# Splitting the down projection's second unit into up's buffers, ahead of up's last sums

## The chip, the cores and the metric

The kernel runs on one core of a Trainium2 chip. The metric is the device time of one execution in microseconds (us); of several runs the median is taken. All times inside an execution are counted from the start of the profiled span.

Engines are called as the profile calls them: PE is TensorE (matmuls), DVE is VectorE, ACT is ScalarE, POOL is GpSimd, SP is SyncE, which here only issues DMAs. ACT and POOL issue DMAs too.

## The reference

One encoder layer over two requests, 512 + 256 = 768 tokens of width 2048, in fp32. A Fourier group and a windowed attention group are mixed and projected, and then comes the part that matters here:

```python
h = rmsnorm(x, ln_mlp_g)
u = relu(h @ w_up)            # (768, 2048) @ (2048, 8192)
x = x + (u * u) @ w_down      # (768, 8192) @ (8192, 2048)
y = rmsnorm(x, ln_final_g)
```

The outputs are the two requests' `y`, fp32.

## The kernel before

Every fp32 product is made of three matmuls in the PE's faster fp32 format. Each factor is split in two, a high part (`wh` for weights, `sh` for the left factor: a copy of the fp32 tile into that format, on ACT) and a low part (`wl`, `sl`: the tile minus its high part, on DVE). A product is high x high + high x low + low x high.

Both projections of the MLP use a Strassen-like scheme with seven products instead of eight, so the factors are sums and differences of quarter matrices.

**Up.** 32 units (numbered 0 to 31, `UL` is the last) of seven steps. In a step, PE makes one of the seven products of the unit (`up_product`), while ACT and DVE prepare the factors of later steps (`up_high`, `up_low`, `up_sum`) and take the results of the previous step (`up_out`): DVE adds the product from PSUM to a partial sum (line 909, "the take"), and in the second half of the units ACT applies relu and square (lines 916 and 917). The four results of a unit are the quarters C11, C12, C22, C21, which end with steps 1, 5, 4 and 6. `up_after` then makes the sums of these quarters that down needs as left factors: C11+C22 after the last step, C12-C11 three steps later, C21-C22 and C11+C21 four steps later. Each is made on DVE (line 923) into one of three `sm` buffers and stored to DRAM (`sd`); in the last unit POOL issues those stores, before it ACT does. For the last unit these later steps fall into the start of down. C12's square is stored too (`a`, line 919).

**Down.** 112 units: two halves of seven products (in the order 4, 2, 6, 0, 1, 3, 5) of eight units each. A unit has one left factor (two of 128 x 384) and two weight tiles of 128 x 1024. `loads(u)` issues the unit's DMAs on SP: the left factor from DRAM (`sr`, line 1128) and the weight tiles (`down_piece`, line 1061). `sums(u)` makes the weight sums where the product needs them, and the high parts (ACT: two `wh` at line 1142, then `sh` at line 1146). `lows(u)` makes the low parts (DVE: two `wl` at line 1152, then `sl` at line 1153). `products(u)` is 36 matmuls on PE (line 1163): for three blocks of rows, two halves of columns, two weight tiles and three terms. In the loop, unit `u` is worked on while unit `u+1`'s `lows`, unit `u+2`'s `sums` and unit `u+3`'s `loads` are issued.

The first eight units of down use product 4, whose weight tiles are kept: they are needed again in later products. `down_piece` puts the kept tiles 0 and 1 into the weight pool's two `raw` buffers (in the profile: `rw`), 2 and 3 into two buffers `re`, and all others into sixteen buffers `rd`.

**Buffers.** Up has a pool of its own, `up`, with four weight buffers `ur` (16 KB per partition in all), two `sx`, ten `o` and three `sm`. It is closed after the last sums, and down's pool `ep` is laid over the same memory: `re` and `sr` over the `ur` buffers, the result tiles `acc0` to `acc11` over `sx`, `o` and `sm`. The buffers `rd` lie over the right factor of up, `xf`, which PE reads until up's last product. A tile laid over another is written only after the last reader of the old one. There are four `wh` and four `wl` buffers in a pool that both stages share.

Unit 0 of down is prepared while up still runs: `loads(0)` at step 3 of the last unit, `sums(0)` and `lows(0)` at step 5. Its left factor is held in three `o` buffers of up (in the profile `osr`, `osh`, `osl`), since the pool `ep` does not exist yet.

**Order.** The order on PE, ACT and DVE is the order of the code. SP and POOL are ordered by the planner at compile time, by when it expects an instruction's inputs and buffers to be ready. The code around the seam, with `up_out(UL, 6)` as the take of C21:

```python
    products(0, ps, 0)
    up_out(UL, 6)
    for m in (1, 2):
        products(0, ps, m)
    for s in (3, 4):
        up_after(UL, s)
    up_ctx.close()
    tctx.close()
```

After it `loads(1)`, `loads(2)` and `sums(1)` follow, and the loop of down starts with `loads(3)` and `lows(1)`. POOL loads the residual into `acc0` to `acc11` (line 1238), four DMAs of 256 KB in each of the loop's iterations 1 to 6.

Of the kernel before, what the change touches and what calls it, by code (L numbers as in the profile page):

```python
# [11 lines left out]
F32 = mybir.dt.float32  # L12
# [8 lines left out]
P = 128  # L21
# [19 lines left out]
def hybrid_encoder(ctx: ExitStack, tc: tile.TileContext, a: dict):  # L41
# [3 lines left out]
    def f32(ap):  # L45
        return ap.bitcast(F32)
# [104 lines left out]
    with ExitStack() as ph:  # L151
# [319 lines left out]
        for pair, c0 in enumerate([0, 256, 512, 768, 2048, 1024, 1280, 1536, 1792]):  # L471
            ps = [[pp.tile([P, 512], F32, tag="ps", name="pz") for _ in range(2)] for _ in range(2)]
            for j in range(4):
                wh, wl = wpiece(w_in[:, 4 * j : 4 * j + 4, c0 : c0 + 256], 4, 256)
# [191 lines left out]
    for u in range(len(units)):  # L666
        t = pace * u
# [258 lines left out]
    def up_out(u, s):  # L926

        if units[u][0] == 0:
            q, bank, how = ((C11, "X", "copy"), (C11, "Z", "add"), (C12, "X", "copy"), (C22, "Y", "copy"), (C22, "X", "add"), (C12, "Y", "add"), (C21, "X", "copy"))[s]
            up_take(u, q, bank, how)  # L930
            if s in (1, 4, 5, 6):
                up_put(u, q)
            return
        q, bank = ((C11, "X"), (C11, "Z"), (C12, "X"), (C22, "Y"), (C22, "X"), (C12, "Y"), (C21, "X"))[s]
        up_take(u, q, bank, "add")
        if s in (1, 4, 5, 6):
            up_relu2(u, q, {C11: s_d[2], C22: s_d[3], C12: a21_d}.get(q))

    def up_after(u, s):


        if u < 0 or units[u][0] == 0:
            return
        if s == 0:
            up_left(u, 0, C11, C22, ALU.add)
        elif s == 3:
            up_left(u, 5, C12, C11, ALU.subtract)
        elif s == 4:
            up_left(u, 6, C21, C22, ALU.subtract)
            up_left(u, 4, C11, C21, ALU.add)  # L950
            for q in range(4):
                del uo[u, q]
# [94 lines left out]

    def down_piece(k, q, h, keep=False):  # L1050

        kk = k % HP
        apart = kk // 4 == (0 if (q, h) == (1, 1) else 1 if (q, h, keep) == (0, 0, True) else -1)
        if apart and kk % 4 < 2:
            raw = wpool.tile([P, 1024], F32, tag="raw", name="rw", bufs=2)
        elif apart:
            raw = ep["p"].tile([P, 1024], F32, tag="re", name="re", bufs=2)
        else:
            raw = ep["p"].tile([P, 1024], F32, tag="rd", name="rd", bufs=16)
        r0 = (4 * (k // 2) + 2 * q + k % 2) * P  # L1060
        nc.sync.dma_start(raw[:], a["w_down"][r0 : r0 + P, h * 1024 : (h + 1) * 1024])
        return raw

    def right_load(i, k):


        if i == 4:
            kept[k] = down_piece(k, 1, 1)
            return kept[k], None
        if i == 2:  # L1070
            return down_piece(k, 0, 1), kept[k]
        if i == 6:
            return down_piece(k, 1, 0), kept[k]
        if i == 0:
            t, kept[k] = kept[k], down_piece(k, 0, 0, True)
            return t, kept[k]
        if i == 1:
            return kept[k], None
        return (down_piece(k, 1, 0), kept[k]) if i == 3 else (down_piece(k, 0, 1), kept.pop(k))
# [35 lines left out]
    def factor_tile(u, what):  # L1115

        dt = F32R if what in ("sh", "sl") else F32
        if u == 0:
            return up.tile([P, 2, HALF], dt, tag="o", name="o" + what, bufs=10)
        return ep["p"].tile([P, 2, HALF], dt, tag=what, name=what, bufs=2 if what == "s2" else 3)  # L1120

    def loads(u):
        kh, i, j = dunits[u]
        g = kh * HP // 2 + j
        srcs = [x[g] for x in left_terms.get(i, (s_d[i],))]
        ss = [factor_tile(u, what) for what, _ in zip(("sr", "s2"), srcs)]
        for x, src in zip(ss, srcs):
            nc.sync.dma_start(x[:], src[:])
        parts[u] = [ss, [right_load(i, kh * HP + 2 * j + q) for q in range(2)]]
# [16 lines left out]
        nc.scalar.activation(sh[:], ss[0][:], AF.Copy)  # L1146
        parts[u] = [(sh, sl, ss[0]), whl]

    def lows(u):
        (sh, sl, sr), whl = parts[u]  # L1150
        for wh, wl, t in whl:
            nc.vector.tensor_tensor(out=wl[:], in0=t[:], in1=f32(wh[:]), op=ALU.subtract)  # L1152
        nc.vector.tensor_tensor(out=sl[:], in0=sr[:], in1=f32(sh[:]), op=ALU.subtract)  # L1153

    def products(u, ps, m, cols=range(2)):
# [20 lines left out]
    kept, parts, ep = {}, {}, {}  # L1176
# [3 lines left out]
    for u in range(len(units)):  # L1180
        for s in range(2 if u == 0 else 0, 7):
            up_step(u, s)
            x2_jobs.get((u, s), lambda: None)()
            if u == 0 and s == 3:
                for x in pts:
                    x1_factors(*x)
                bctx.close()
            if u == 13 and s == 0:
                xs = up_ctx.enter_context(tc.tile_pool(name="xs", bufs=1, side="right", reuse_waits="tile")).tile([P, 2, 4, HALF], F32R, tag="xs", name="xs")
                nc.gpsimd.dma_start(f32(xs[:]), x2_d[steps[0][1]][:])  # L1190
                right.append([xs])
            if u == UL and s == 3:
                loads(0)
            if u == UL and s == 5:
                sums(0)
                lows(0)
            if u == UL and s == 6:
                up_after(UL, 0)
    ps = [pp.tile([P, 2, 512], F32, tag="ps", name="pd") for _ in range(3)]
    ps = [x[:].rearrange("p a b -> p (a b)") for x in ps]  # L1200
    products(0, ps, 0)
    up_out(UL, 6)
    for m in (1, 2):
        products(0, ps, m)
    for s in (3, 4):
# [15 lines left out]
        acc[i // 2][i % 2] = epool.tile([P, 1024], F32, tag=f"acc{i}", name=f"acc{i}")  # L1221
    acc4 = lambda m, n: acc[m][n // 2][:, n % 2 * 512 : (n % 2 + 1) * 512]
    ep["gf"] = epool.tile([P, D], F32, tag="gf", name="gf")
    loads(1)
    loads(2)
    sums(1)
    behind = None
    for u, (kh, i, j) in enumerate(dunits):
        if j == 0 and u > 0:
            ps = [pp.tile([P, 2, 512], F32, tag="ps", name="pd") for _ in range(3)]  # L1230
            ps = [x[:].rearrange("p a b -> p (a b)") for x in ps]
        final = kh == 1 and i == order[-1]
        last = j == HP // 2 - 1
        if u + 3 < len(dunits):
            loads(u + 3)
        if 1 <= u <= NM:
            for n in range(4):
                nc.gpsimd.dma_start(acc4(u - 1, n), x1_d[u - 1][n][:])
        if u == NM + 1:
            nc.gpsimd.dma_start(ep["gf"][:], a["ln_final_g"].partition_broadcast(P))  # L1240
        if u + 1 < len(dunits):
            lows(u + 1)
        if final:
            for fn in beside[j]:
                fn()

        def evacuate(m, ns=None, i=i, ps=ps):
            for r, c, sign in results[i]:
                x, y = acc[3 * r + m][c][:], ps[m]
                if ns is not None:  # L1250
                    x, y = x[:, ns * 512 : (ns + 1) * 512], y[:, ns * 512 : (ns + 1) * 512]
                sc = rm if sign > 0 else nrm
                nc.vector.scalar_tensor_tensor(
                    out=x, in0=y, scalar=sc[:, 3 * r + m : 3 * r + m + 1], in1=x, op0=ALU.mult, op1=ALU.add
                )

        for m in range(3 if u > 0 else 0):

            if not (final and j >= HP // 2 - 2 and m == 2):
                products(u, ps, m)  # L1260
        if final and last:
            for n in range(2):
                for v in (u - 1, u):
                    products(v, ps, 2, (n,))

            for what, m, q in (
# [3 lines left out]
            ):  # L1270
                if what == "e":
                    evacuate(m, q - 2)
                    square(3 + m, q)
                elif what == "g":
                    for n in range(2):
                        gains(3 + m, n)
                elif what == "r":
                    row_factor(3 + m)
                else:
                    put(3 + m, q, q < 2, {(2, 0): nc.gpsimd, (2, 1): nc.scalar}.get((m, q), nc.sync))  # L1280
            parts.clear()
        if not (final and j >= HP // 2 - 2):
            del parts[u]
        if behind is not None:
            behind(2)
            behind = None
        if u + 2 < len(dunits):
            sums(u + 2)
        if last and not final:
            evacuate(0)  # L1290
            evacuate(1)
            behind = evacuate
# [58 lines left out]
```

## Time and profile before

| what | value |
|---|---|
| median of 3 runs | 2660.26 us (2658.65 to 2661.46) |
| profiled execution: span from first to last instruction | 2660.9 us |
| profiled execution: its own time | not given apart from the span |
| PE busy | 2606.8 us, 98% |
| DVE, ACT, POOL busy | 1732.0, 1060.1, 265.1 us |
| DMA | 468.31 MB, mean 176 GB/s |
| matmuls of up (line 888) | 781 to 1727 us |
| matmuls of down (line 1163) | 1726.8 to 2648 us |

How to read the lines further down. A row of the timeline is: start, duration, engine, line of the kernel, operation, output <- inputs, shapes, count; in brackets the idle time of that engine just before it, and what ended it. "ACTq" or "SPq" is the issue of a DMA on that engine's queue. A row of the chain is: start, duration, what the end of the execution waited for in that stretch. A row of the waits is: who, at which line, <- for what: total us, times, longest. In a row of stretches, the busy times of PE, PE's weight loads, DVE, ACT and POOL follow the length, each with its count, then the granted clock of PE (1.00 is full), the busy share of the DMA engines and GB/s.

### The profile page before, as it was taken

Reading aid. Unit: us, or ns where it says so; the run is one execution under the profiler, and the core shown is the slowest. Engines: PE = TensorE matmul, PEld = TensorE weight load, DVE = VectorE, ACT = ScalarE, POOL = GpSimd, SP = SyncE. Lnnn points to the kernel's source line nnn. Section 1 sums busy time; section 2 is a strip of 40 time slices with the busy share of each in tenths; the row PEclk is TensorE's granted clock in tenths of the full one; section 3 lists DMA queues with packets and bytes.
Section 4 is the critical chain, followed back from the end, with each engine's and each line's share of the span. In section 5 each row is a group of like instructions: output and inputs, shape, how many; then the busy total and the mean of one; then the engine's idle time right before and its main releaser. Section 6 shows DMA issues by size and latency. Waiting matters only on the chain.

```text
span 2660.9 us, 35017 instructions
## 1 busy us (share of the span) xinstructions
PE 2606.8 (98%) x13652; PEld 2376.5 (89%) x13652; DVE 1732.0 (65%) x2100; ACT 1060.1 (40%) x1523; POOL 265.1 (10%) x375
## 2 busy tenths in 40 slices
PE   8999998998999999998999999999999999999998
PEld 8999997877889999998999999978888888888886
DVE  6334446766746565654777777747776775777677
ACT  5233326664433333332545444433333333333335
POOL 1011212334210010101000000020000000000000
PEclk9999999999999999999999999999999999999999
DMA  5323464444664454547666666585553672554364
GB/s 172 122 93 109 140 202 146 121 127 150 205 219 159 157 188 160 182 151 278 199 227 231 212 217 230 188 326 178 178 176 99 203 255 65 180 186 157 102 206 145
DMA packets 261094, 468.31 MB, mean 176 GB/s; under 512 B 26240, under 2 KB 157824, under 8 KB 259392
## 3 DMA queue, kind: packets, MB, share of 16 engines
q1 hardware_dynamic: 196064, 304.83, 36.3%
q10 hardware_dynamic: 51792, 101.73, 9.9%
q0 software_dynamic: 13072, 59.52, 6.4%
q8 instruction: 107, 1.75, 0.3%
q14 instruction: 59, 0.48, 0.1%
HBM read 345.67 MB, written 120.32 MB: 175 GB/s over the span
## 4 chain that ended last, share of the span: by engine, by line
PE 88%; DMA 4%; DVE 3%; issue 3%; ACT 1%; POOL 1%; SPq 0%; POOLq 0%; ACTq 0%; DVEq 0%
PE pd L1163 34%; PE pu L888 32%; PE pz L481 11%; PE pm L693 6%; PE pv L186 1%; DMA ur<-in_w_up 1%; PE pa L313 1%; PE s L522 1%; PE o L596 1%; PE t L577 1%; DMA oar<-oad 0%; PE pe L334 0%; DMA ry<-zq 0%; DVE s L535 0%; ACT p L552 0%
## 5 line engine op out<-in xcount | busy, mean ns | idle before, releaser
L888 PE MATMUL pu<-xf,wh 128*128 128x384 f32 x3328 | 850.4, 337 | 8.4 <-ACT wh L868 6.8
L888 PEld LDWEIGHTS pu<-xf,wh 128*128 128x128 f32 x3328 | 601.9, 188 | 11.1 <-ACT wh L868 7.2
L888 PE MATMUL pu<-xf,wl 128*128 128x384 f32 x1664 | 559.9, 336 | 0.3 <-DVE wl L874 0.3
L1163 PE MATMUL pd<-wl,sh 128*128 128x512 f32 x1332 | 519.3, 390 | 2.7 <-DVE wl L1152 2.7
L1163 PE MATMUL pd<-wh,sl 128*128 128x512 f32 x1332 | 519.5, 390 | 1.5 <-DVE sl L1153 1.5
L1163 PE MATMUL pd<-wh,sh 128*128 128x512 f32 x1332 | 519.4, 390 | 0.0
L1142 ACT ACTIVATE wh<-rd 128x1024 fp32r<-128x1024 f32 x200 | 202.0, 1054 | 532.5 <-PE pd L1163 441.9
L1152 DVE TENSOR_TENSOR wl<-rd,wh 128x1024 fp32r<-128x1024 f32 x200 | 236.0, 1221 | 235.6 <-ACT wh L1142 235.0
L868 ACT ACTIVATE wh<-ur 128x1024 fp32r<-128x1024 f32 x160 | 169.9, 1062 | 385.2 <-PE pu L888 198.6
L888 PEld LDWEIGHTS pu<-xf,wl 128*128 128x128 f32 x1664 | 313.2, 188 | 0.8 <-DVE wl L874 0.8
L1163 PEld LDWEIGHTS pd<-wl,sh 128*128 128x128 f32 x1332 | 250.7, 188 | 55.3 <-DVE wl L1152 3.1
L1163 PEld LDWEIGHTS pd<-wh,sl 128*128 128x128 f32 x1332 | 250.7, 188 | 54.1 <-DVE sl L1153 1.8
L1163 PEld LDWEIGHTS pd<-wh,sh 128*128 128x128 f32 x1332 | 250.7, 188 | 51.9
L874 DVE TENSOR_TENSOR wl<-ur,wh 128x1024 fp32r<-128x1024 f32 x160 | 195.6, 1222 | 94.9 <-ACT wh L868 94.9
L909 DVE TENSOR_TENSOR o<-pu,o 128x768 f32<-128x768 f32 x160 | 153.0, 956 | 116.0 <-PE pu L888 112.3
L481 PE MATMUL pz<-hh,wh 128*128 128x384 f32 x576 | 147.0, 336 | 0.0
L481 PE MATMUL pz<-hh,wl 128*128 128x384 f32 x576 | 146.2, 334 | 0.0
L481 PE MATMUL pz<-hl,wh 128*128 128x384 f32 x576 | 146.1, 334 | 0.0
L1135 DVE TENSOR_TENSOR rd<-rd 128x1024 f32<-128x1024 f32 x112 | 131.8, 1218 | 0.0
L868 ACT ACTIVATE wh<-sx 128x1024 fp32r<-128x1024 f32 x64 | 67.9, 1062 | 129.2 <-PE pu L888 99.4
L66 DVE TENSOR_TENSOR wl<-raw,wh 128x1024 fp32r<-128x1024 f32 x56 | 69.0, 1236 | 66.6 <-ACT wh L65 64.0
L1153 DVE TENSOR_TENSOR sl<-sr,sh 128x768 fp32r<-128x768 f32 x111 | 105.6, 951 | 0.0
(209 smaller groups left out, 3564.5 us busy)
## 6 DMA issues: line engine op xcount, KB each, us to landing
rd<-in_w_down SPq DMA_DIRECT2D x176, 512.0 KB, 5.1
ur<-in_w_up SPq DMA_DIRECT2D x128, 512.0 KB, 3.8
sr<-sd SPq DMA_DIRECT2D x95, 384.0 KB, 5.4
pd<-o ACTq DMA_DIRECT2D x64, 384.0 KB, 2.3
o<-pd POOLq DMA_DIRECT2D x64, 384.0 KB, 6.0
sd<-sm ACTq DMA_DIRECT2D x60, 384.0 KB, 2.8
raw<-in_w_in SPq DMA_DIRECT2D x40, 512.0 KB, 3.6
raw<-in_w_out SPq DMA_DIRECT2D x32, 512.0 KB, 4.8
```

Of the source, the lines that this page charges most:

```text
L66: nc.vector.tensor_tensor(out=lo, in0=src, in1=f32(hi), op=ALU.subtract)
L481: nc.tensor.matmul(ps[c][s][:, :HALF], w[:, i, cs], h[j][:, i, s * HALF : (s + 1) * HALF], start=first and n == 0, stop=last and n == 2,)
L693: nc.tensor.matmul(ps[:], l(k), w[:, k % 2, :], start=(k == 0 and n == 0), stop=(k == 7 and n == 2))
L868: nc.scalar.activation(wh[:], raw[:], AF.Copy)
L874: nc.vector.tensor_tensor(out=wl[:], in0=raw[:], in1=f32(wh[:]), op=ALU.subtract)
L888: nc.tensor.matmul(ps[:, t, :HALF], w[:, i, t * P : (t + 1) * P], xb[:, o, i, :], start=(s == first_of[bank] and i == 0 and n == 0), stop= ...
L909: nc.vector.tensor_tensor(out=o, in0=src, in1=o, op=ALU.add)
L1135: add = lambda x, y, op: nc.vector.tensor_tensor(out=x[:], in0=x[:], in1=y[:], op=op)
L1142: nc.scalar.activation(wh[:], t[:], AF.Copy)
L1152: nc.vector.tensor_tensor(out=wl[:], in0=t[:], in1=f32(wh[:]), op=ALU.subtract)
L1153: nc.vector.tensor_tensor(out=sl[:], in0=sr[:], in1=f32(sh[:]), op=ALU.subtract)
L1163: nc.tensor.matmul(ps[m][:, ns], l[:, q, ts], w[:, ns], start=(j == 0 and q == 0 and t == 0), stop=(j == HP // 2 - 1 and q == 1 and t == 2),)
```

## The change

Unit 1 of down is prepared while up still runs, as unit 0 was.

- `loads(1)` moves to step 5 of the last unit of up, behind `lows(0)`. Its left factor goes into three more `o` buffers of up, and its two weight tiles (numbers 2 and 3) into two of up's `ur` buffers (`down_piece(..., early=True)`, tag `ur`, named `rw`).
- `sums(1)` and the first `wl` of `lows(1)` move to step 6, behind the sum C11+C22. The second `wl` and the `sl` come behind the take of C21, in front of up's last three sums.
- Tiles 2 and 3 are kept for later products, but up's buffers do not last; so they are loaded a second time into `re`, after `loads(2)`.
- The loop leaves out `lows(1)`, which is done.

```diff
@@ def down_piece
-    def down_piece(k, q, h, keep=False):
+    def down_piece(k, q, h, keep=False, early=False):
...
-        if apart and kk % 4 < 2:
+        if early:
+            raw = up.tile([P, 1024], F32, tag="ur", name="rw", bufs=4)
+        elif apart and kk % 4 < 2:
@@ def right_load
+        if i == 4 and k in (2, 3):
+            return down_piece(k, 1, 1, early=True), None
         if i == 4:
             kept[k] = down_piece(k, 1, 1)
             return kept[k], None
@@ def factor_tile
-        if u == 0:
+        if u < 2:
             return up.tile([P, 2, HALF], dt, tag="o", name="o" + what, bufs=10)
@@ def lows
-    def lows(u):
+    def lows(u, qs=range(2)):
         (sh, sl, sr), whl = parts[u]
-        for wh, wl, t in whl:
+        for wh, wl, t in [whl[q] for q in qs]:
             nc.vector.tensor_tensor(out=wl[:], in0=t[:], in1=f32(wh[:]), op=ALU.subtract)
+        if 1 not in qs:
+            return
         nc.vector.tensor_tensor(out=sl[:], in0=sr[:], in1=f32(sh[:]), op=ALU.subtract)
@@ the last unit of up
             if u == UL and s == 5:
                 sums(0)
                 lows(0)
+                loads(1)
             if u == UL and s == 6:
                 up_after(UL, 0)
+                sums(1)
+                lows(1, (0,))
...
     products(0, ps, 0)
     up_out(UL, 6)
+    lows(1, (1,))
     for m in (1, 2):
         products(0, ps, m)
@@ after up's pools are closed
-    loads(1)
     loads(2)
-    sums(1)
+    for k in (2, 3):
+        kept[k] = down_piece(k, 1, 1)
...
-        if u + 1 < len(dunits):
+        if 0 < u and u + 1 < len(dunits):
             lows(u + 1)
```

## The prediction

> **What bounds the kernel now.** I read the page's busy times first, then the chain in order of time, then PE's waits, then each engine's instructions around the place where the chain leaves PE between the up and the down projection.
>
> ```profile
> PE 2606.8 (98%) x13652; PEld 2376.5 (89%) x13652; DVE 1732.0 (65%) x2100; ACT 1060.1 (40%) x1523; POOL 265.1 (10%) x375
> ```
>
> PE is the bound, with 98% busy. So only time in which PE stands still or runs slowly can be won.
>
> ```profile
> 1728.17 7.56 DMA sd<-sm
> ...
> 1739.97 891.51 PE pd L1163 x3919
> ```
>
> This is the chain in order of time (start, us, what). At the seam it leaves PE for a store of `sm` and sums of VectorE; from 1739.97 to 2631 it is PE alone. The waits say what PE stood for (total, times, longest):
>
> ```profile
> PE pd L1163 <- DVE wl L1152: 2.7, 1, 2.7
> PE pd L1163 <- DVE sl L1153: 1.5, 1, 1.5
> ```
>
> They are PE's only waits from 1700 to 2631. The instructions of PE there:
>
> ```profile
> 1726.76 0.39 PE L1163 MATMUL pd<-wh,osh 128*128 128x512 f32 x1
> ...
> 1734.92 0.39 PE L1163 MATMUL pd<-wh,sh 128*128 128x512 f32 x1
> 1737.97 0.50 PE L1163 MATMUL pd<-wl,sh 128*128 128x512 f32 x1 [2.66 <-DVE wl L1152]
> 1739.97 0.80 PE L1163 MATMUL pd<-wh,sl 128*128 128x512 f32 x1 [1.50 <-DVE sl L1153]
> ...
> 1746.39 0.40 PE L1163 MATMUL pd<-wh,sl 128*128 128x512 f32 x1
> ...
> 1750.71 0.39 PE L1163 MATMUL pd<-wh,sh 128*128 128x512 f32 x1
> ```
>
> Unit 0 of down (36 matmuls) runs from 1726.76 to 1734.92: 8.16 us, 0.2267 each. Unit 1 runs from 1734.92 to 1750.71, the first matmul of unit 2: 15.79 us for the same 36. The seam costs **15.79 - 8.16 = 7.63 us**. Of that, 3.05 + 2.00 - 2 x 0.2267 = 4.60 is standing still, and the 15 starts from 1739.97 to 1746.39 take 6.42 instead of 3.40, 3.02 more: the clock was low.
>
> ```profile
> 1726.76:1734.92 8.16, 8.16 (x38) 6.76 (x37) 3.90 (x5) 6.50 (x8) 1.64 (x3) 1.00 0.81 252
> 1739.97:1746.39 6.42, 6.42 (x15) 5.08 (x16) 3.09 (x3) 0.00 (x0) 2.97 (x6) 0.51 0.96 355
> 1744.00:1759.00 15.00, 15.00 (x63) 12.33 (x62) 3.23 (x3) 3.35 (x4) 6.46 (x12) 0.93 1.03 418
> ```
>
> (Stretch; after the busy times the granted clock, the DMA share and GB/s.) Granted clock 1.00 before the gap, 0.51 behind it.
>
> **The change, part by part.** Why was unit 1 late? VectorE and ScalarE, in order:
>
> ```profile
> 1727.79 0.95 DVE L909 TENSOR_TENSOR o<-pu,o 128x768 f32<-128x768 f32 x1
> ...
> 1735.82 0.96 DVE L923 TENSOR_TENSOR sm<-o 128x768 f32<-128x768 f32 x1 [3.94 <-DMA sd<-sm]
> 1736.70 2.35 DVE L1152 TENSOR_TENSOR wl<-re,wh 128x1024 fp32r<-128x1024 f32 x2
> 1738.97 0.95 DVE L1153 TENSOR_TENSOR sl<-sr,sh 128x768 fp32r<-128x768 f32 x1
> ```
>
> ```profile
> 1728.80 0.33 ACTq L919 DMA_DIRECT2D a<-o  x1
> 1729.17 0.85 ACT L916 ACTIVATE o<-o 128x768 f32<-128x768 f32 x1 [0.40 <-ACT o L917]
> ...
> 1730.80 1.99 ACT L1142 ACTIVATE wh<-re 128x1024 fp32r<-128x1024 f32 x2
> 1732.69 0.83 ACT L1146 ACTIVATE sh<-sr 128x768 fp32r<-128x768 f32 x1
> 1734.44 2.00 ACT L1142 ACTIVATE wh<-rd 128x1024 fp32r<-128x1024 f32 x2 [0.92 <-PE pd L1163]
> ```
>
> Unit 1's `lows` (two `wl`, one `sl`) are queued on VectorE behind up's last sum, which waits 3.94 us for one of the three `sm` buffers, whose store lands at 1728.17 + 7.56 = 1735.73. On ScalarE its `wh` and `sh` stand behind C21's relu and square (from 1729.17).
>
> *The splits moved ahead.* On ScalarE `sums(1)` (two `wh`, one `sh`) comes in front of C21's relu and square. It can start where that relu started, 1729.17: the `wh` end at 1730.23 and 1731.17, `sh` at 1732.0. On VectorE the first `wl` follows at 1730.3 to 1731.5, the take of C21 (0.95) to 1732.4, the second `wl` to 1733.5, `sl` to 1734.4 (1.22 and 0.95 each, overlapping by some 0.08 as in the rows). PE wants them at 1734.92 (first), 1735.15 (`wl`) and 1735.37 (`sl`). So `sl` is **1.0 us early**, the others more. Gain: the 4.60, and with no gap no low clock: 3.02. I take 7.6. The new wait of the first `wl` (for 1730.23) holds the take of C21 behind it, and so C21's PSUM buffer until 1732.4; in the code the next to use it is down's second group, unit 8, due at 1792.
>
> *What moves back.* C21's relu and square (0.85 each) go from 1729.17 to 1732.4, end by 1734.1, and unit 2's `wh` still starts at 1734.44, where it waits for PE. The three last sums run 1734.4 to 1737.0; the third no longer waits, since its buffer is free at 1735.73. Behind them are unit 2's `lows`: 1737.0 plus 2.35 plus 0.95 is 1740.2. PE wants unit 2 at 1734.92 + 8.16 = 1743.08, so 2.9 us are left. GpSimd's stores of these sums go out at about 1735.3, 1736.2 and 1737.1, and its loads of `acc`, queued behind, begin as before:
>
> ```profile
> 1737.08 0.54 POOL L924 DMA_DIRECT2D sd<-sm  x1 [4.36 <-DVE sm L923]
> 1737.61 4.25 POOL L1238 DMA_DIRECT2D acc<-x  x8
> ```
>
> Four of the `acc` tiles lie over `o` buffers that unit 1 now holds until PE has done it (1743.1); their loads are the 11th and later, and at 0.53 each the 11th is due at 1742.9 at the earliest, so the hold is 0.2 us, of tiles wanted first at unit 7's end, 1792.
>
> *The moved loads.* `osr` and two `rw` of unit 1 go into up's buffers. SyncE can issue them when unit 30's last sum has freed an `o` buffer, about 1717.2; they replace one `sr` and two `re` of the same sizes. The nearest load, the `sr` of 1716.6 below, landed 6.8 us after issue: so by 1725, a few tenths of issue included; ScalarE wants them at 1729.17. Cost 0; cover 4 us.
>
> *The two tiles loaded twice.* 2 x 512 KB more. They lie over a buffer of unit 1, so SyncE holds at them until VectorE has read it (1731.5 or 1733.5), with unit 3's loads behind. This meets a stretch in which the DMA engines are full (418 GB/s, above):
>
> ```profile
> 1726.95 0.81 SPq L1061 DMA_DIRECT2D rd<-in_w_down  x2
> ...
> 1737.32 0.81 SPq L1061 DMA_DIRECT2D rd<-in_w_down  x2
> ```
>
> Loads issued near 1716, 1737 and 1743, with the time from issue to landing:
>
> ```profile
> L1128 SPq DMA_DIRECT2D sr<-sd x1: 327/327/327, 1716.6 to 1716.6; - x1
> DMA to landing us min/median/max: 6.8/6.8/6.8
> L1061 SPq DMA_DIRECT2D rd<-in_w_down x2: 328/380/433, 1737.3 to 1737.7; - x2
> DMA to landing us min/median/max: 4.3/5.4/6.6
> L1061 SPq DMA_DIRECT2D rd<-in_w_down x2: 457/470/482, 1743.5 to 1744.0; - x2
> DMA to landing us min/median/max: 13.0/14.0/15.0
> ```
>
> Unit 2's tiles (1726.95) stand ahead of the reload and keep their time. Unit 3's second tile lands at 1737.7 + 6.6 = 1744.3, unit 5's at 1744.0 + 15.0 = 1759.0; between them come 2 x (2 x 512 + 384) KB (the tiles' sizes by the code), so SyncE's queue gets 196 GB/s: 7.4 us for a unit that PE works on for 8.16. From below, the reload fits before 1737.6 and costs 0. From above, its 1 MB is moved at 196 GB/s ahead of unit 3: 5.3 us, landing 1749.6; then `wh` 1.06, `wl` 1.22 and `sl` 0.88 reach 1752.8, where PE wants `sl` at 1734.92 + 2 x 8.16 + 0.45 = 1751.7: PE stands 1.1 us. Later units gain 0.8 each. I take 0, since SyncE waited until 1737.32 before and now has unit 3's loads ready to go some 2 us sooner.
>
> The trace has the split by row; a page has it by rule. The Trainium skill, "DMA: Bandwidth & Descriptors", section on queues, rings and completion order, says that each DMA engine takes turns between the queues that have work, packet by packet. Half of 418 would be 209 GB/s, an estimate from that rule; by it the reload costs 5.0 us of lead, and the sum stays the same within the 1.1 us above.
>
> *The rest* (buffer names, the order of `lows`) costs nothing: the number of sums and activations is unchanged.
>
> Sum: -4.60 - 3.02 + 0 = **-7.6 us**. The profiled span of 2660.9 stands 0.6 above the median of the runs, 2660.26; against the median this is **2652.6 us** (-0.29%). About 0.2%, 5.3 us, is what a measurement of this kernel can tell from no change.
>
> **The rivals.** *Unit 3 or 4 starved.* Reload and bunched stores push unit 3 later than the bound above: issued at 1736 with the 15.0 us of unit 5's tile it lands at 1751.0, `sl` is there at 1754.2, and PE stands 2.5 us. A short stand costs itself only:
>
> ```profile
> 1269.07 0.59 PE L888 MATMUL pu<-xf,wh 128*128 128x384 f32 x2 [1.52 <-issue]
> ...
> 1269.67 0.51 PE L888 MATMUL pu<-xf,wh 128*128 128x384 f32 x2
> ```
>
> After 1.52 us of standing the next pairs take 0.59 and 0.51, the usual time. So 2655.1. For it: the full DMA engines. Against it: 196 GB/s is more than PE uses, and unit 3's second tile landed 1758.9 - 1744.3 = 14.6 us ahead of its PE time.
>
> *The moved loads late, a wait in the place of the one removed.* If unit 1's tiles, issued at 1718.4, took those 15.0 us, they land at 1733.4, the `wh` end at 1735.4, `sl` at 1737.5: PE stands 2.2 us, 2654.8. Against it: DMA has room there, and the rows show 6.8.
>
> *Slower: the queue order.* SyncE's order is left to the compile-time planner. If it puts the reload ahead of unit 2's tiles, these go out at 1733.9 instead of 1726.95. The point that decides: PE then stands from 1743.8 (second tile), low clock adds 3.0, and the gain is gone once it stands over 4.6 us, when the tiles land after some 1746. At the longest landing of any `rd` load (the last number),
>
> ```profile
> DMA to landing us min/median/max: 3.0/5.1/17.2
> ```
>
> 17.2 us, they land at 1751.1, the products can go on at 1753.4, PE stands 9.6, and 9.6 + 3.0 - 7.6 = +5.0: 2665.3. Against it: in the code unit 2's loads come first, and the reload is ready later.
>
> A sentence apart: the Trainium skill, "TensorE: Matmul & The Clock Gate", Part 1, gives a cold stretch of about 3.4 us at half rate, an estimated loss of 1.7 where the rows have 3.02; by the page the gap would be worth 6.3 instead of 7.6, and the rows decide.
>
> **How the numbers follow.** Forecast 0.70, unit 3 starved 0.12, moved loads late 0.06, queue order 0.07, unforeseen of either sign 0.05. The forecast's own range is 2651.2 to 2654.2 (the runs spread 1.4 to either side). The range is 2651.0 to 2657.0: it takes in both partial gains and leaves out the queue order, the unforeseen and the forecast's lower edge. Faster by over 0.2% (below 2654.9): 0.70, half of the two partial cases, 0.09, less 0.01: 0.78. Within 0.2%: the other half and most of the queue order, whose 2665.3 lies at that bound: 0.15. Slower: 0.07.
>
> **What would show it.** In the profile after: PE's waits at its L1163 gone; unit 1 as long as unit 0 (8.16 us); granted clock near 1.00 through the seam; `wl` of unit 1 read from `rw`, ahead of the last three sums; the last sum without its wait for a store; unit 2's `sl` done by about 1740; from 1744 on everything 7.6 us earlier. The prediction is wrong if PE stands at unit 2, 3 or 4 for `wl` or `wh` behind a late `rd`, or if a low clock shows behind a gap that I have at zero.

## The result, and the profile after

Over eight runs of each, the changed kernel takes 2653.78 us (2651.6 to 2654.89) and the kernel before 2659.88 (2657.5 to 2662.11). The ratio is **0.9975, with a 95% interval of 0.9966 to 0.9985**: faster by 6.6 us by the ratio, between 4 and 9, and by 6.1 us by the medians. A second series gave 2653.34 against 2659.08, ratio 0.9976 (0.9967 to 0.9984).

The forecast was 2652.6, range 2651 to 2657. The question was where a gain of this size comes from, and whether the reload gives part of it back.

The page and the chain after:

```profile
span 2651.5 us, 35021 instructions
...
PE 2602.9 (98%) x13652; PEld 2374.7 (90%) x13652; DVE 1726.5 (65%) x2100; ACT 1059.8 (40%) x1523; POOL 264.1 (10%) x375
```

```profile
1267.23 457.86 PE pu L888 x2640
1725.09 896.93 PE pd L1169 x3957
```

The chain (start, us, what) now runs from up into down without leaving PE. PE has no wait at all between 1690 and the end of down's products. Units 0, 1 and 2 of down, as stretches, starting at down's first matmul:

```profile
1724.93 0.39 PE L1169 MATMUL pd<-wh,osh 128*128 128x512 f32 x1
```

```profile
1724.93:1733.09 8.16, 8.16 (x38) 6.76 (x37) 5.77 (x7) 6.62 (x8) 0.55 (x1) 1.00 0.84 278
1733.09:1741.25 8.16, 8.16 (x38) 6.76 (x36) 5.19 (x6) 2.26 (x3) 4.28 (x8) 1.00 0.98 339
1741.25:1749.41 8.16, 8.16 (x38) 6.76 (x36) 3.32 (x3) 3.26 (x4) 3.22 (x6) 1.00 1.02 418
```

Unit 1 takes 8.16 us where it took 15.79, PE is busy throughout, and the granted clock stays at 1.00. VectorE at the seam:

```profile
1728.43 1.23 DVE L1156 TENSOR_TENSOR wl<-rw,wh 128x1024 fp32r<-128x1024 f32 x1 [2.39 <-ACT wh L1146]
1729.58 0.95 DVE L909 TENSOR_TENSOR o<-pu,o 128x768 f32<-128x768 f32 x1
1730.45 1.21 DVE L1156 TENSOR_TENSOR wl<-rw,wh 128x1024 fp32r<-128x1024 f32 x1
1731.58 0.95 DVE L1159 TENSOR_TENSOR osl<-osr,osh 128x768 fp32r<-128x768 f32 x1
1732.45 2.69 DVE L923 TENSOR_TENSOR sm<-o 128x768 f32<-128x768 f32 x3
1735.05 2.35 DVE L1156 TENSOR_TENSOR wl<-rd,wh 128x1024 fp32r<-128x1024 f32 x2
1737.33 0.95 DVE L1159 TENSOR_TENSOR sl<-sr,sh 128x768 fp32r<-128x768 f32 x1
```

Unit 1's three low parts end at 1732.53, ahead of the three sums, which run back to back: the wait for a store is gone.

**A measure that leaves out the scatter.** Down's first matmul starts at 1726.76 in the profile before and at 1724.93 after, though PE's work ahead of it is the same; over all profiles of this study it lies between 1723.28 and 1728.30, in no order with the kernels. Why it scatters is not known. So I compare the stretch from that matmul to the end of the span: 2660.9 - 1726.76 = 934.1 before, 2651.5 - 1724.93 = 926.6 after, **7.5 us less**. The stretch has a scatter of its own, mostly from the low clock behind a stand of PE: the kernel before gave 933.3 in a second profile (6.7 us), and kernel b, further down, 929.3 to 931.0. All kernels on this measure (the two columns on the left are the row of the first matmul and the page's span):

```
kernel                                   first     span    stretch  over the change   ratio (95%)
before                                   1726.76   2660.9  934.1    +7.5              1
before, again                            1723.99   2657.3  933.3    +6.7              -
the change                               1724.93   2651.5  926.6     0                0.9975 (0.9966-0.9985)
the change, again                        1728.30   2654.8  926.5    -0.1              0.9976 (0.9967-0.9984)
a: free buffer for the last sum          1727.09   2654.3  927.2    +0.6              0.9982 (0.9973-0.9990)
f: a, and low parts reordered            1725.20   2652.0  926.8    +0.2              0.9982 (0.9973-0.9991)
b: low parts behind the sums             1725.93   2656.9  931.0    +4.4              0.9991 (0.9982-1.0000)
b again                                  1724.27   2653.6  929.3    +2.7              -
b a third time                           1727.18   2658.2  931.0    +4.4              -
c: reload after unit 7's loads           1723.28   2649.8  926.5    -0.1              0.9979 (0.9970-0.9987)
d2: two more tiles loaded                1727.55   2660.5  933.0    +6.4              1.0003 (0.9994-1.0012)
d4: four more tiles loaded               1725.21   2662.1  936.9    +10.3             1.0017 (1.0008-1.0027)
e: reload ahead of unit 2's loads        1724.20   2655.1  930.9    +4.3              0.9988 (0.9979-0.9998)
```

### The profile page after: what moved, and what is told of

It is laid out like the page before. It is cut to its first block, busy times and chain, and to the rows that moved or that the text cites. A ratio compares the mean times of both kernels' runs of the same rounds, so it can differ in the third digit from the quotient of the medians.

```text
span 2651.5 us, 35021 instructions
## 1 busy us (share of the span) xinstructions
PE 2602.9 (98%) x13652; PEld 2374.7 (90%) x13652; DVE 1726.5 (65%) x2100; ACT 1059.8 (40%) x1523; POOL 264.1 (10%) x375
## 4 chain that ended last, share of the span: by engine, by line
PE 90%; DMA 3%; DVE 3%; POOL 1%; ACT 1%; issue 1%; SPq 0%; POOLq 0%; ACTq 0%; DVEq 0%
PE pu L888 34%; PE pd L1169 34%; PE pz L481 11%; PE pm L693 6%; PE pv L186 1%; DMA ur<-in_w_up 1%; PE pa L313 1%; PE o L596 1%; PE s L522 1%; DMA ofr<-ofd 1%; PE t L577 1%; PE pe L334 0%; ACT p L552 0%; DMA oar<-oad 0%; PE ptx L131 0%
## 5 line engine op out<-in xcount | busy, mean ns | idle before, releaser
L1169 PE MATMUL pd<-wh,sh 128*128 128x512 f32 x1320 | 513.5, 389 | 0.0
L1169 PE MATMUL pd<-wl,sh 128*128 128x512 f32 x1320 | 513.5, 389 | 0.0
L1169 PE MATMUL pd<-wh,sl 128*128 128x512 f32 x1320 | 513.5, 389 | 0.0
```

The costliest lines, as they stand in the source:

```text
L1169: nc.tensor.matmul(ps[m][:, ns], l[:, q, ts], w[:, ns], start=(j == 0 and q == 0 and t == 0), stop=(j == HP // 2 - 1 and q == 1 and t == 2),)
```

## The experiments

**The wait for the buffer alone (a).** From the kernel before:

```diff
-        sm = up.tile([P, 2, HALF], F32, tag="sm", name="sm", bufs=3)
+        if u == len(units) - 1 and i == 4:
+            sm = up.tile([P, 2, HALF], F32, tag="o", name="so", bufs=10)
+        else:
+            sm = up.tile([P, 2, HALF], F32, tag="sm", name="sm", bufs=3)
```

> The kernel before with one edit: the last of up's sums (C11+C21) takes a free o buffer in place of the third-round sm buffer, so it need not wait 3.94 us for a store. Unit 1 stays where it was, with no early buffers and no reload. Theory (unit 1's low parts were late because they stood behind that wait on VectorE): the low parts start at about 1732.7 instead of 1736.7, sl is done at 1735.9, 0.5 us after PE wants it; PE stands 0.5 us, no low clock, gain 7.1 us, ratio 0.9973. Rival (it takes the move into up's buffers to close the gap, the wait is only the last of several): PE still stands 2 us or more and the clock falls, gain under 4 us, ratio above 0.9985.

PE's only wait in down, and VectorE ahead of it:

```profile
PE pd L1166 <- DVE sl L1156: 0.4, 1, 0.4
```

```profile
1732.13 0.95 DVE L926 TENSOR_TENSOR so<-o 128x768 f32<-128x768 f32 x1
1733.00 2.35 DVE L1155 TENSOR_TENSOR wl<-re,wh 128x1024 fp32r<-128x1024 f32 x2
1735.27 0.95 DVE L1156 TENSOR_TENSOR sl<-sr,sh 128x768 fp32r<-128x768 f32 x1
```

The stretch is 927.2: 6.9 of the 7.5 us come from one buffer (6.1 of 6.7 against the second profile of before), with no early load, no reload and unit 1 where it was. The theory's size (7.1) holds and the rival falls on the stretch; the ratio of 0.9982 is nearer to the rival's bound of 0.9985, and its interval holds both.

**The rest of it (f).** On top of a, in `lows` for unit 1 alone, `sl` between the two `wl`:

```diff
-        for wh, wl, t in whl:
+        for q, (wh, wl, t) in enumerate(whl):
+            if u == 1 and q == 1:
+                nc.vector.tensor_tensor(out=sl[:], in0=sr[:], in1=f32(sh[:]), op=ALU.subtract)
             nc.vector.tensor_tensor(out=wl[:], in0=t[:], in1=f32(wh[:]), op=ALU.subtract)
+        if u == 1:
+            return
```

> The kernel before with the free o buffer for the last sum, and unit 1's low parts in the order wl, sl, wl. No early buffers, no reload. Theory (the gap is the order and the one buffer wait on VectorE, nothing else): sl comes 1.1 us earlier than in the kernel with the free buffer alone, where PE stood 0.4 us for it; PE stands 0.1 us or not at all, from the first matmul of down to the end as long as the changed kernel (926.6 us, against 934.1 before), ratio 0.9972 to 0.9977. Rival (the early buffers bring something of their own): 1 us or more longer than the changed kernel over that stretch.

```profile
1731.11 1.22 DVE L1157 TENSOR_TENSOR wl<-re,wh 128x1024 fp32r<-128x1024 f32 x1
1732.24 0.95 DVE L1156 TENSOR_TENSOR sl<-sr,sh 128x768 fp32r<-128x768 f32 x1
1733.11 1.22 DVE L1157 TENSOR_TENSOR wl<-re,wh 128x1024 fp32r<-128x1024 f32 x1
```

No wait of PE at down is left, and the stretch is 926.8, 0.2 above the change. The median, 2653.41, is that of the change beside it, 2653.34, to 0.1 us; the ratio, 0.9982, lies outside what I expected, with an interval that holds nearly all of it (0.9973 to 0.9991). So a kernel without early buffers and without 1 MB more of loads closes nearly the same gap. It does not beat the change.

**The order on VectorE (b, three profiles).** In the changed kernel, one line moved back:

```diff
-    lows(1, (1,))
     for m in (1, 2):
         products(0, ps, m)
     for s in (3, 4):
         up_after(UL, s)
+    lows(1, (1,))
```

> The changed kernel with one line moved back: the second wl and the sl of unit 1 stand behind up's last three sums again; early loads, early wh, sh and first wl stay. Theory (the order on VectorE is what counts): the last sum waits for its buffer until about 1735.7 (on the clock of before), wl and sl end at 1738.8, PE stands 3.4 us. If a stand of 3.4 us brings the low clock, 6.4 of 7.6 us are given back, ratio 0.9995; if it does not, 3.4 are given back, ratio 0.9985. Rival (ScalarE's part, moved ahead of C21's relu and square, is what counts): PE stands under 1 us, ratio as the change, 0.9972 to 0.9975.

```profile
PE pd L1169 <- DVE osl L1159: 2.5, 1, 2.5
```

```profile
1733.32 1.83 DVE L923 TENSOR_TENSOR sm<-o 128x768 f32<-128x768 f32 x2 [0.93 <-ACT o L917]
1735.07 1.22 DVE L1156 TENSOR_TENSOR wl<-rw,wh 128x1024 fp32r<-128x1024 f32 x1
1736.20 0.95 DVE L1159 TENSOR_TENSOR osl<-osr,osh 128x768 fp32r<-128x768 f32 x1
```

The gap is back, so early loads and an early ScalarE are not enough; the rival falls. The stand is 2.5 and not 3.4 us, because the last sum had its buffer without a wait here: the store that frees it landed 5.5 us after issue, where it had taken 7.56 in the kernel before.

```profile
L924 POOL DMA_DIRECT2D sd<-sm x1: 548/548/548, 1727.3 to 1727.3; - x1
DMA to landing us min/median/max: 5.5/5.5/5.5
```

The change has the same 5.5, and a has 7.5 us; why is not tested. A low clock followed. To see how long it is, the same kernel ran twice more, and the kernel before once more:

> The kernel with the low parts behind the sums, profiled once more. In its first profile PE stood 2.5 us and the low clock began 0.9 us after PE had gone on, for seven starts, 1.7 us lost; a stand of 2.7 us in the kernel with two extra loads cost 3.5. Theory (the stand sets it): 2.5 us and 1.7 us again, 931.0 us from the first matmul of down to the end. Rival (a window decides): another start and another length, 929.2 to 933 us.

> The same kernel a third time, for the same question. Theory: 2.5 us of standing, 1.7 us by the low clock, 931.0 us. Rival: 929.2 to 933 us, unlike the run before it.

> The kernel before, unchanged, profiled once more, to see whether the low clock behind the seam's gap has a fixed length. Theory (the stand sets it): stand 2.7 and 1.5 us as in the first profile, low clock from 15 starts, loss 3.0 us, first matmul of down to the end 934.1 us. Rival (the length of the low clock depends on where the gap falls in some window of the clock's control): the same stand, but a loss of 1 to 4 us by the low clock, so 932 to 935 us.

The three profiles of b over the same stretch (PE busy first, then the granted clock after the busy times):

```profile
1732.00:1750.00 18.00, 15.50 (x61) 12.36 (x61) 9.15 (x10) 6.71 (x8) 8.55 (x16) 0.91 1.00 368
```

```profile
1732.00:1750.00 18.00, 15.50 (x69) 12.52 (x68) 9.49 (x10) 5.54 (x6) 8.57 (x16) 1.00 0.99 362
```

```profile
1732.00:1750.00 18.00, 15.51 (x62) 12.34 (x61) 9.83 (x10) 5.95 (x8) 8.05 (x15) 0.91 0.99 360
```

PE stands 2.5 us in all three, and the clock is 0.91, 1.00, 0.91: in the second there was no low clock at all, and that profile is the one that is 1.7 us shorter. In the kernel before, run again, the stands were 2.38 and 1.41 us instead of 2.66 and 1.50, and the low clock cost 2.4 us instead of 3.0:

```profile
PE pd L1163 <- DVE wl L1152: 2.4, 1, 2.4
PE pd L1163 <- DVE sl L1153: 1.4, 1, 1.4
```

Its stands were not quite equal to the first profile's, so that pair alone would not decide. The three of b do, and the rival holds: the stand does not fix the low clock's length. That a window of the clock's control decides is a guess that fits; these runs do not show a window.

**The reload: later, first, and with more bytes (c, e, d2, d4).** In the changed kernel:

```diff
 c: the two reloads from behind loads(2) into the loop:
+        if u == 4:
+            for k in (2, 3):
+                kept[k] = down_piece(k, 1, 1)
 e: the two reloads in front of loads(2)
 d2, d4: behind the reloads, with (8, 9) or (8, 9, 10, 11):
+    for k in (8, 9, 10, 11):
+        down_piece(k, 0, 1)
```

> The changed kernel with the two reloads issued after unit 7's loads instead of ahead of unit 3's. Theory (DMA has room for the reload): PE was never starved, so the time is that of the change, ratio 0.9972 to 0.9976; only ScalarE's wait for unit 3's tiles shrinks, from 2 us to none. Rival (the reload gives back the 1 to 1.5 us by which the measured gain fell short of 7.6): 1 us or more faster than the change, ratio 0.9970 or below, and PE's stretch of down's first eight units shorter than in the change.

ScalarE at unit 3, in the change and in c:

```profile
1741.63 1.06 ACT L1146 ACTIVATE wh<-rd 128x1024 fp32r<-128x1024 f32 x1 [6.28 <-DMA rd<-in_w_down]
1744.66 1.06 ACT L1146 ACTIVATE wh<-rd 128x1024 fp32r<-128x1024 f32 x1 [1.97 <-DMA rd<-in_w_down]
```

```profile
1739.12 2.01 ACT L1146 ACTIVATE wh<-rd 128x1024 fp32r<-128x1024 f32 x2 [5.42 <-PE pd L1169]
```

In the change ScalarE waits for unit 3's tiles; in c it waits for PE, as in a steady state. The stretch is the same to 0.1 us. So the reload costs nothing, and nothing of the gain is given back there; the rival falls. (The ratio, 0.9979, is above the expected 0.9976, on the side away from the rival's 0.9970; its interval of 0.9970 to 0.9987 alone would not decide.)

> The changed kernel with four more tiles of 512 KB loaded (and not used) between the reload and unit 3's loads, a threefold reload. Theory (the reload is hidden, but only by the lead that unit 3's tiles have, some 2 us in the changed kernel): at 196 to 209 GB/s for SyncE's queue, 2 MB put unit 3's second tile 10 to 10.7 us later, PE stands about 8 us at unit 3 and the low clock adds 3: 11 us slower than the change, ratio about 1.0015. Rival (these loads have room to spare in any amount): as the change, ratio 0.9975.

> The changed kernel with two more tiles of 512 KB between the reload and unit 3's loads. With four, unit 3's second tile landed 10.9 us later, 2.7 us for a tile. Theory (linear in the bytes, and the changed kernel has 2.0 us of lead at unit 3): two put it 5.4 us later, to 1750.0; sl is done at 1753.3 where PE wants it at 1749.9, PE stands 3.4 us, and the low clock adds 1.7 as behind the stand of 2.5: 5 us slower than the changed kernel, ratio 0.9994. Rival (a lead of more than 2 us, for instance because GpSimd's queue yields): under 1.5 us.

First PE and ScalarE with four tiles, then ScalarE with two:

```profile
1757.48 0.80 PE L1169 MATMUL pd<-wh,sh 128*128 128x512 f32 x1 [7.63 <-ACT sh L1150]
```

```profile
1753.15 1.06 ACT L1146 ACTIVATE wh<-rd 128x1024 fp32r<-128x1024 f32 x1 [17.51 <-DMA rd<-in_w_down]
1755.64 1.06 ACT L1146 ACTIVATE wh<-rd 128x1024 fp32r<-128x1024 f32 x1 [1.44 <-DMA rd<-in_w_down]
```

```profile
1753.04 1.06 ACT L1146 ACTIVATE wh<-rd 128x1024 fp32r<-128x1024 f32 x1 [1.50 <-DMA rd<-in_w_down]
```

Counted from down's first matmul, unit 3's second tile is there at 19.7 us in the change (1744.66 - 1724.93), at 25.5 with two more tiles and at 30.4 with four: 5.8 us for 1 MB, 10.7 for 2 MB, so 182 to 196 GB/s for SyncE's queue, an estimate that takes the whole delay for the transfer of the added bytes (the queue's own bytes, further down, give 203 to 212). PE stands 2.7 + 0.2 us with two tiles and 7.6 + 0.2 with four; the rest of the +6.4 and +10.3 us, 3.5 and 2.5, is low clock. For two tiles I had expected a longer stand (3.4) and a shorter low clock (1.7), 5 us in all. So the change has a lead of some 2 us at unit 3: enough for its own reload, not for 1 MB more.

> The changed kernel with the reload ahead of unit 2's loads in SyncE's queue, the queue order of my slower rival. Theory (the order of that queue decides, since it holds until VectorE has read the early buffers): unit 2's tiles go out some 5.5 us later, behind 1 MB, and land as unit 3's do in the changed kernel, 10 to 12 us after issue, near 1743; PE stands 4 to 5 us for unit 2, with the low clock 6.5 to 8 us in all, ratio 0.9995 to 1.0005. Rival (the reload costs nothing wherever it stands): under 1 us, ratio as the changed kernel.

```profile
1728.96 0.80 SPq L1063 DMA_DIRECT2D re<-in_w_down  x2
1729.81 0.42 SPq L1132 DMA_DIRECT2D sr<-sd  x1
1730.48 0.89 SPq L1063 DMA_DIRECT2D rd<-in_w_down  x2
```

```profile
1742.36 0.50 PE L1169 MATMUL pd<-wh,sh 128*128 128x512 f32 x1 [1.67 <-ACT sh L1150]
1742.69 0.40 PE L1169 MATMUL pd<-wl,sh 128*128 128x512 f32 x1
1743.75 0.80 PE L1169 MATMUL pd<-wh,sl 128*128 128x512 f32 x1 [0.66 <-DVE sl L1159]
```

Unit 2's tiles go out at 1730.48, 6.3 us after down's first matmul (0.2 before), and land after 7.6 and 9.6 us. PE stands 2.3 us (1.67 + 0.66) instead of 4 to 5; with the low clock 4.3 are lost. The mechanism is right, its size was too high: the order of two pairs of loads on one queue is worth more than half of the gain on the stretch.

**The change once more.**

> The changed kernel once more, beside the others of this group. Theory: from the first matmul of down to the end 926.6 us, no wait of PE at down; the time before down's first matmul (1724.9 in the first profile, 1726.8 in the kernel before) scatters from run to run by some 2 us either way and has nothing to do with the change, so the ratio lies at 0.9972, for 7.5 us. Rival (1 to 1.5 us of the 7.6 are given back somewhere): the stretch is 927.5 us or longer, ratio 0.9977.

Its stretch, 926.5, agrees to 0.1 us with the first, so nothing is given back inside down. The ratio of 0.9976 cannot tell 6.4 from 7.5 us.

## Why the prediction was right, point by point

- *What bounds the kernel.* The gap of unit 1 was the only stand of PE between 1700 and down's end, and closing it moved the time. Right.
- *The splits moved ahead.* `sl` of unit 1 was put at 1734.4, 7.6 us after down's first matmul; it ended at 1732.53, also 7.6 after. Unit 2's `sl`, put at 13.4, came at 13.35. Rows of durations, laid behind one another by the code's order, gave these to 0.1 us.
- *Standing still, 4.60 us.* Gone entirely. Experiments a and b place it: 6.9 of 7.5 us (the low clock behind the stand included) hang on the one wait for an `sm` buffer, and with all else moved but the last two low parts, 2.5 us of standing come back.
- *Low clock, 3.02 us.* Right in kind, and the term whose size was not fixed. The kernel before, run again, lost 2.4; b lost 1.7, 0 and 1.7 behind equal stands. The 7.6 is therefore the upper end of what the stretch shows (6.7 and 7.5), and the runs' 6.6 us, between 4 and 9, agrees with it.
- *The moved loads.* The planner put unit 1's two weight tiles into SyncE's queue at 1673.42 and 1682.36, some 40 us earlier than I said, since their buffers were free (the first landed 3.3 us after issue). They did not stand behind `osr`, which went out at 1714.55. The cost, 0, was right; the rival of late loads could not happen for the weights.
- *The reload.* I took 0 between bounds of 0 and 5.3 us of delay. Unit 3's second tile came 2.1 us later than before (19.7 after the first matmul, against 1744.3 - 1726.76 = 17.5), and PE had 2.0 us to spare: `sl` at 1747.85 where PE wanted it at 1749.86. My reason, that unit 3's loads are issued sooner, was true (7.1 us after the first matmul against 10.6) but they stood in the queue: these took 9.5 and 11.9 us to land, against 4.3 and 6.6 before. The upper bound of 5.3 us, less the 3.4 by which these loads were issued sooner, is 1.9, an estimate close to the 2.1 measured: both halves of the working were right, but together they leave a delay of some 2 us, not of 0. The 0 in the time holds because PE had the 2.0 us left over.

```profile
L1063 SPq DMA_DIRECT2D rd<-in_w_down x2: 586/709/832, 1732.1 to 1732.7; - x2
DMA to landing us min/median/max: 9.5/10.7/11.9
```

- *The rivals.* Starving did not occur, and d2 shows that it stood one megabyte away. The queue order, made to happen in e, costs 4.3 and not 12.6 us: I had priced it with the longest landing of any such load, 17.2, and it was 9.6. The change would have stayed faster. The two partial rivals were priced too low: from one row, a stand of 1.52 us without a low clock, I took it that stands of 2.5 and 2.2 us cost only themselves. Behind the stand of 2.5 us in b the low clock took 1.7 us more in two of three profiles, and behind 2.7 + 0.2 us in d2 it took 3.5.
- *The rule on the DMA queues.* The half share of 209 GB/s that I worked out from the Trainium skill, "DMA: Bandwidth & Descriptors", section on queues, rings and completion order, is borne out where the added loads run beside GpSimd's. The bytes of SyncE's queue (q1) and GpSimd's (q0), from 1740 to 1753 in d2 and from 1740 to 1755 in d4:

```profile
q1 hardware_dynamic: 827, 2.76, 52.5%
q0 software_dynamic: 677, 2.64, 49.4%
```

```profile
q0 software_dynamic: 899, 3.23, 52.7%
q1 hardware_dynamic: 904, 3.05, 49.8%
```

(Packets, MB, share of the DMA engines.) SyncE's queue moved 212 and 203 GB/s, 51% and 49% of the two. The 182 to 196 from the delays is lower, so the delay was not transfer alone; what else it holds is open.

## What to carry to other kernels

When PE stands at a seam between two stages, lay the queue of the engine that releases it out in order and look for the one instruction with a wait of its own: everything behind it is late by that wait, though its inputs are there. Here one spare buffer for the last sum was worth 6.9 us of 7.5, and moving a whole unit's preparation across the seam, with a reload, was worth the other 0.6, of which f got 0.4 by reordering three instructions. Before adding loads next to a seam, work out the lead of the next unit's tiles: it was 2 us, and 1 MB more ate 6.4 us of the 7.5 (d2).

## What the runs showed of the hardware

- Behind equal stands of 2.5 us PE lost 1.7, 0 and 1.7 us to the low clock (b). It need not begin when PE goes on: in the first profile of b PE ran 0.90 us at a granted clock of 0.87 before it fell to 0.52, and in the third 1.54 us at 0.96 before 0.51.

```profile
1737.21:1738.11 0.90, 0.90 (x4) 0.71 (x5) 0.90 (x1) 0.00 (x0) 0.90 (x3) 0.87 1.10 391
1738.11:1741.42 3.31, 3.31 (x9) 2.63 (x8) 2.18 (x3) 0.00 (x0) 1.20 (x3) 0.52 0.98 367
```

```profile
1738.44:1739.98 1.54, 1.53 (x6) 1.24 (x7) 1.54 (x2) 0.00 (x0) 1.45 (x3) 0.96 1.06 388
1739.98:1743.35 3.37, 3.37 (x10) 2.67 (x8) 1.55 (x2) 0.00 (x0) 1.28 (x3) 0.51 0.97 353
```

- A stand of 0.4 us (a) and one of 1.5 us (in up) brought no low clock, in one profile each; in e one came behind 1.67 and 0.66 us with two matmuls between them.
- The low clock can last longer than the stand: behind 2.7 us in d2 it went on from 1754.88 to 1761.56, over 6 us, with a further stand of 0.2 in it.

```profile
1754.88:1761.56 6.68, 6.50 (x15) 4.68 (x16) 3.29 (x4) 2.85 (x3) 2.69 (x5) 0.50 1.03 419
```

- The Trainium skill, "TensorE: Matmul & The Clock Gate", Part 1, gives the window as about 3.4 us and free-running. That equal stands differ agrees with a free-running window; that a stand of 2.5 us was enough, and that the low clock lasted over 6 us, does not follow from its figure for one window.
- Two DMA queues with work moved half of the bytes each in d2 and d4, where their packets were alike, 3.3 to 3.9 KB on average. They did not where the packets differed: in the kernel before, from 1231 to 1259 us, GpSimd's queue had packets of some 9 KB and SyncE's of 1 KB, and SyncE's got 1.43 of 11.54 MB, though it moved more packets.

```profile
q0 software_dynamic: 1073, 9.70, 82.9%
q1 hardware_dynamic: 1425, 1.43, 14.6%
```

- The time before down's first matmul differed by up to 5.0 us between profiles (1723.28 to 1728.30). For effects of this size, a stretch inside the profile told more than the time of a run: 33 runs of the kernel before spread from 2655.99 to 2664.29, while the stretch agreed to 0.1 us in two profiles of the change, where PE never stood, to 0.8 in two of the kernel before and to 1.7 in three of b.
